# Issuing the scores of the next attention task before the PV of this one, and splitting each scan step into two group halves

## The chip, the cores and the metric

The kernel runs on the 8 cores of one Trainium2 chip. Each core computes 4 of the 32 sequences. The metric is device time in microseconds of the slowest core. PE is TensorE, PEld its weight loads, DVE VectorE, ACT ScalarE, POOL GpSimd and SP SyncE. A program on all cores also has a slower state, in which one die is granted a lower clock (in one run of e1 0.71 of full speed, against 0.77 on the other die); all comparisons here use fast runs only.

## The reference, cut to what matters

The model has four layers. Each runs a bidirectional complex-diagonal state-space scan beside a banded attention of window 128, and then a ConvFFN.

```python
# attention: 16 query blocks of 128, up to 3 key blocks each, 2 kv heads x 4 query heads
s = jnp.einsum('bnqkgd,bnskd->bnkgqs', q, kb) * (HEAD_DIM ** -0.5)
...
p = e / (jnp.sum(e, axis=-1, keepdims=True) + jnp.exp(sink_l - m))
o = jnp.einsum('bnkgqs,bnskd->bnqkgd', p, vb)
# scan, forward and reverse, 32 groups x 64 states
s_t = a * s_{t-1} + B u_t        # complex, real and imaginary parts kept apart
```

The kernel cuts the 2048 tokens into 64 chunks. Pass A (matrix multiplies) gives each chunk's contribution. The carry then runs through 64 dependent steps on DVE. Pass B adds the result back.

## The kernel before

Every instruction goes through a helper, which turns the buffers named as `reads` and `writes` into semaphore waits. A DVE operation that names a buffer which the previous DVE operation wrote waits for it, though both are on one engine. An attention "task" is one pair (query block `qb`, kv head `kv`).

```python
def att_block(qb):
    for kv in range(2):
        for kb in kbs:                       # 2 or 3 key blocks
            # S:   psum <- kT, qT                 PE   L822
            # exp: et   <- psum                   ACT  L825
            # pt   <- et * bias table             DVE  L827
        for c in range(4):                   # PV: 12 matmuls, PE L834
            ...
        # den <- psum + sink; den <- 1/den; oa <- psum*den     DVE L839, L841, L842
    # square of oa (ACT L845), 4 transposes (PE L849), copy to yaT (ACT L851)

def scan_step(c):      # L856 to L859; H is [128, 2 (re/im), 32 groups, 65 chunks]
    st1 = H[:, :, :, c] * aL[:, 0]           # every operation names the same buffer,
    H[:, :, :, c + 1] += st1                 # so each one waits for the one before it
    st1 = H[:, ::-1, :, c] * aL[:, 1]
    H[:, :, :, c + 1] += st1

for qb in range(8):                          # first half of the stage
    att_block(qb)
    passA_batch(4 * qb)      # 32 matmuls over 4 groups (L873); 2 mAb weight buffers from DRAM;
                             # two ACT copies put the result into H (L882, L883)
for qb in range(8, 16):                      # second half
    att_block(qb)
    for c in ...: scan_step(c)               # 8 steps a block
# then Ein <- H (DVE L896), pass B and the rest
```

The softmax here doesn't subtract the row's maximum and nothing guards it: scores larger than these inputs give would overflow.

## Time and profile before

| | |
|---|---|
| median before the change | 26421.76 us (6 runs) |
| the stage, first sequence: first H copy to Ein | 1143.22 to 1398.94 = 255.7 us, 16 times in the program |
| first half: pitch from block to block | 15.15 us on average |
| second half: pitch from block to block | 18.39 us is the usual value, 18.75 the longest |

Pitches are read from the timeline: in the first half the start of the first H copy of each block, in the second the start of every other reciprocal of den.

The overall view of the page, kernel before (the profiled run's span is 26406.8 us): busy us of each engine, share of the span, instructions.

```profile
PE 14588.9 (55%) x84876; PEld 8215.1 (31%) x84876; DVE 12674.6 (48%) x22475; ACT 8765.8 (33%) x14892; POOL 2825.2 (11%) x2532
```

No engine is near full, because the program is a row of stages with different limits. So the stage itself must be looked at. This is its window view, kernel before: the stretch and its length, then busy us of each engine with the instruction count, granted TensorE clock, DMA share and GB/s.

```profile
1143.22:1249.24 106.02, 58.48 (x463) 34.48 (x462) 28.54 (x84) 39.35 (x77) 0.00 (x0) 0.50 0.24 74
1249.24:1398.94 149.70, 47.36 (x262) 21.67 (x260) 98.04 (x351) 35.85 (x72) 0.00 (x0) 0.50 0.01 5
```

Nothing is full in the first half either: PE is busy 58 of 106 us. What bounds it is a chain through several engines. One stretch of the chain of waits, kernel before (start, length, what):

```profile
1207.89 0.55 PE psum L822
1208.64 0.61 ACT et_88 L825
1209.34 0.42 DVE pt_91 L827
...
1210.89 0.72 PE psum L834 x10
...
1212.93 1.09 PE psum L849 x4
...
1215.35 3.05 DMA mAb_84<-matsA
```

S, exp, multiply, PV and transposes follow each other, each begun when the one before has ended (the lines left out between PV and the transposes are den, its reciprocal and oa), and PE only works in between. The last line is a wait of PE for pass-A weights.

The second half is DVE's. Its timeline, kernel before, from the end of a scan into the attention work:

```profile
1325.06 0.27 DVE L858 TENSOR_TENSOR st_81<-H,aL 128x64 f32<-128x64 f32 x1
1325.43 0.28 DVE L859 TENSOR_TENSOR H<-H,st_81 128x64 f32<-128x64 f32 x1
1325.61 0.41 DVE L827 TENSOR_TENSOR pt_94<-et_88,eb 128x512 bf16<-128x512 bf16 x1
1325.94 0.42 DVE L827 TENSOR_TENSOR pt_95<-et_89,eb 128x512 bf16<-128x512 bf16 x1
...
1327.65 0.16 DVE L839 TENSOR_TENSOR den_98<-psum,esink 128x4 f32<-128x4 f32 x1 [0.96 <-PE psum L834]
...
1328.99 0.42 DVE L827 TENSOR_TENSOR pt_91<-et_88,eb 128x512 bf16<-128x512 bf16 x1 [0.36 <-ACT et_88 L825]
```

Two things are to be seen. The scan operations last 0.27 us but start every 0.37: each waits 0.10 for the one before. The multiplies after them last 0.42 but start every 0.33, because they do not depend on each other. And DVE stands idle (0.96 us for PV, 0.36 for exp, and 0.97 for the second PV, not shown).

### The profile page before, as it was taken

The numbers are of one execution on the slowest core, as the hardware profiler recorded it, in microseconds if no ns is written. First come the engines' busy times: TensorE is split into PE (matmuls) and PEld (weight loads), VectorE is DVE, ScalarE is ACT, GpSimd is POOL, SyncE is SP. The second block draws the span as 40 slices with busy tenths as digits, with TensorE's granted clock in tenths as the row PEclk, the third lists the DMA queues.
The fourth block names the chain that finished last, engine by engine and source line by source line (L and its number), as shares of the span: only waits on it lengthen the run. The fifth ranks groups of instructions, "written<-read, shape, count | busy, mean of one in ns | idle before, by whom it ended". The sixth has DMA issues, their size and how long they took to land.

```text
span 26406.8 us, 296755 instructions; the slowest of 8 cores (26307.9 to 26406.8 us)
## 1 busy us (share of the span) xinstructions
PE 14588.9 (55%) x84876; PEld 8215.1 (31%) x84876; DVE 12674.6 (48%) x22475; ACT 8765.8 (33%) x14892; POOL 2825.2 (11%) x2532
## 2 busy tenths in 40 slices
PE   1355437777235553777724555377772445537777
PEld 0222214444122221444412222244441222224444
DVE  7533435555653333555564333355557443335555
ACT  1333323444133332434413333244341333324443
POOL 1100001111210000111120000011112000001111
PEclk8666669999656666999965666699996566669999
DMA  0232231111022323111102222311110222231111
GB/s 28 71 90 86 85 115 42 36 38 40 33 66 90 90 87 119 34 37 40 34 33 71 85 90 90 117 37 39 35 38 33 81 76 84 90 117 40 40 37 35
DMA packets 664396, 1668.09 MB, mean 63 GB/s; under 512 B 115568, under 2 KB 248352, under 8 KB 654496
## 3 DMA queue, kind: packets, MB, share of 16 engines
q1 hardware_dynamic: 643808, 1558.92, 18.8%
q10 hardware_dynamic: 19008, 90.19, 1.1%
q8 instruction: 737, 12.08, 0.2%
q14 instruction: 843, 6.91, 0.1%
HBM read 1211.89 MB, written 436.99 MB: 62 GB/s over the span
## 4 chain that ended last, share of the span: by engine, by line
DVE 32%; PE 22%; DMA 19%; issue 13%; ACT 12%; DVEq 1%; ACTq 1%; SPq 0%; POOL 0%; POOLq 0%
PE psum L1084 10%; PE psum L1172 4%; DVE qT L942 2%; DMA z_scr<-hTlo 2%; PE psum L918 2%; DMA UY<-u_scr 2%; PE psum L834 1%; DVEq L97 1%; ACT fjunk L1120 1%; DVE H L857 1%; DVE H L859 1%; PE psum L822 1%; PE psum L873 1%; PE psum L745 1%; DMA xt_680<-out 1%
## 5 line engine op out<-in xcount | busy, mean ns | idle before, releaser
L1172 PE MATMUL psum<-h2T,wu 128*128 128x386 bf16 (+1 forms) x33792 | 5306.1, 311 | 1627.3 <-DVE cv_606 L1182 140.5
L1172 PEld LDWEIGHTS psum<-h2T,wu 128*128 128x128 bf16 x33792 | 3170.4, 98 | 3764.8 <-issue 2281.7
L1084 PE MATMUL psum<-wd,gbuf 128*128 128x512 bf16 x9216 | 2151.0, 389 | 26.7 <-POOL gbuf L1188 26.7
L1084 PEld LDWEIGHTS psum<-wd,gbuf 128*128 128x128 bf16 x9216 | 923.6, 100 | 1185.4 <-issue 152.4
L822 PE MATMUL psum<-qT,kT 64*128 64x512 bf16 x1472 | 708.9, 614 | 0.0
L979 PE MATMUL psum<-wo,hThi 128*128 128x512 bf16 x2048 | 507.8, 393 | 324.8 <-DVE mt_783 L984 13.6
L1092 DVE RECIPROCAL fstd<-fstd 128x1 f32<-128x1 f32 x256 | 41.9, 164 | 1297.8 <-ACT fstd L1090 1290.8
L1088 ACT ACTIVATE fjunk<-psum 128x1024 bf16<-128x1024 f32 x256 | 261.5, 1022 | 1197.0 <-PE psum L1084 1197.0
L769 PE MATMUL psum<-hTlo,wi 128*128 128x512 bf16 x2304 | 612.0, 389 | 44.6 <-DVE hTlo L748 16.5
L769 PE MATMUL psum<-hThi,wi 128*128 128x512 bf16 x2304 | 606.1, 386 | 0.0
L973 PE MATMUL psum<-wo,qT 128*128 128x512 bf16 x2048 | 519.1, 399 | 133.6 <-ACT mt_128 L982 5.1
L922 ACT ACTIVATE hTlo<-psum 128x512 bf16<-128x512 f32 x256 | 152.9, 597 | 1233.8 <-PE psum L918 1233.6
L778 DVE CAST qT<-psum 128x512 bf16<-128x512 f32 x256 | 177.0, 691 | 797.3 <-PE psum L769 797.3
L904 DVE MEMSET psum<- 128x512 f32 x256 | 124.2, 485 | 663.7 <-ACT hTlo L922 655.8
L979 PEld LDWEIGHTS psum<-wo,hThi 128*128 128x128 bf16 x2048 | 192.8, 100 | 629.5 <-issue 447.0
L1188 POOL TENSOR_TENSOR gpre_597<-gg_610,cv_604 128x384 bf16<-128x384 f32 (+1 forms) x24 | 21.8, 907 | 3332.9 <-ACT gg_610 L1185 3332.9
L1188 POOL TENSOR_TENSOR gpre_395<-gg_408,cv_402 128x384 bf16<-128x384 f32 (+1 forms) x24 | 21.8, 907 | 3329.7 <-ACT gg_408 L1185 3329.7
L1188 POOL TENSOR_TENSOR gpre_799<-gg_812,cv_806 128x384 bf16<-128x384 f32 (+1 forms) x24 | 21.8, 907 | 3326.2 <-ACT gg_812 L1185 3326.2
L1188 POOL TENSOR_TENSOR gpre_193<-gg_206,cv_200 128x384 bf16<-128x384 f32 (+1 forms) x24 | 21.8, 907 | 3319.9 <-ACT gg_206 L1185 3319.9
L769 PEld LDWEIGHTS psum<-hTlo,wi 128*128 128x128 bf16 x2304 | 224.7, 100 | 344.0 <-issue 98.9
L973 PEld LDWEIGHTS psum<-wo,qT 128*128 128x128 bf16 x2048 | 194.2, 101 | 438.3 <-issue 260.9
L1143 ACT CAST h2T<-psum 128x512 bf16<-128x512 f32 (+1 forms) x272 | 155.3, 571 | 523.9 <-DVE h2T L1141 523.9
(1963 smaller groups left out, 33605.7 us busy)
## 6 DMA issues: line engine op xcount, KB each, us to landing
UY<-u_scr SPq DMA_DIRECT2D x128, 256.0 KB
z_scr<-hTlo SPq DMA_DIRECT2D x128, 256.0 KB
xt_73<-x SPq DMA_DIRECT2D x56, 512.0 KB
xt_275<-out SPq DMA_DIRECT2D x56, 512.0 KB
xt_477<-out SPq DMA_DIRECT2D x56, 512.0 KB
xt_679<-out SPq DMA_DIRECT2D x56, 512.0 KB
fxt_196<-out SPq DMA_DIRECT2D x55, 512.0 KB
fxt_197<-out SPq DMA_DIRECT2D x55, 512.0 KB
```

The costliest lines, as they stand in the source:

```text
L97: E.eng.wait_ge(sem, val)
L745: K.op(pe, lambda: nc.tensor.transpose(psum[:, b + c // 4, (c % 4) * 128:(c % 4 + 1) * 128], hs[i][:, c * 128:(c + 1) * 128], ident[:]), r ...
L769: K.op(pe, lambda: nc.tensor.matmul(psum[:, b, :], wi[:, k, m * 128:(m + 1) * 128], hT[k // 4][:, k % 4, tg * 512:(tg + 1) * 512], start=( ...
L822: K.op(pe, lambda: nc.tensor.matmul(psum[:, b, :], kT[rows, kb * 128:(kb + 1) * 128], qT[rows, :, qb * 128:(qb + 1) * 128], start=True, st ...
L834: K.op(pe, lambda: nc.tensor.matmul(psum[:, b, c * 65:(c + 1) * 65], pt[ip][:, c * 128:(c + 1) * 128], vaug[:, kb, kv, 0:65], start=(n_ == ...
L857: K.op(dve, lambda: V.tensor_tensor(out=H[:, :, :, c + 1], in0=H[:, :, :, c + 1], in1=st1[:], op=ALU.add), reads=[H_b, aL_b, Hf_b], writes ...
L918: K.op(pe, lambda: nc.tensor.matmul(o_, l_, r_, start=False, stop=(n_ == len(mm) - 1), skip_group_check=True), reads=[mBb_b[im]] + rd_, wr ...
L942: K.op(dve, lambda: V.tensor_tensor(out=nat(ysT), in0=X1[:, m, tg * 512:(tg + 1) * 512].rearrange("p (s sub) -> p s sub", s=2), in1=gate[i ...
L973: K.op(pe, lambda: nc.tensor.matmul(psum[:, ba + hf, :], ysT[:, k, tt * 128:(tt + 1) * 128], wo[:, k, hf * 512:(hf + 1) * 512], start=(k = ...
L979: K.op(pe, lambda: nc.tensor.matmul(psum[:, bb_ + hf, :], yaT[:, k, tt * 128:(tt + 1) * 128], wo[:, 4 + k, hf * 512:(hf + 1) * 512], start ...
L1084: K.op(pe, lambda: nc.tensor.matmul(psum[:, b + hf, :], gt_[:, gi_, ti * 128:(ti + 1) * 128], wd[:, fb, hf * 512:(hf + 1) * 512], start=(f ...
L1172: K.op(pe, lambda: nc.tensor.matmul(psum[:, b, 0:nW], wu[:, k, rb * 128:(rb + 1) * 128], h2T[:, k, w0c:w1c], start=(k == 0), stop=(k == 7) ...
```

## The change

The intent is to give each in-order engine other work while a chain is in flight. Attention is cut into three parts: `att_S` (S, exp, multiply), `att_P` (PV, den, oa) and `att_F` (square, transposes, copy). The S part of the next task is issued before the PV part of this one, and the final part one task later. The scan step works on two halves of the groups in alternation.

```diff
-        for qb in range(NT // 2):
-            att_block(qb)
-            passA_batch(4 * qb)
+        tasks = [(qb, kv) for qb in range(NT) for kv in range(2)]
...
+        cur = att_S(*tasks[0])
+        fin = None
+        for ti, (qb, kv) in enumerate(tasks):
+            nxt = att_S(*tasks[ti + 1]) if ti + 1 < len(tasks) else None
+            att_P(qb, kv, cur)
+            cur = nxt
+            if fin is not None:
+                att_F(fin)
+                fin = None
+            if kv == 1:
+                fin = qb
+                if qb < NT // 2:
+                    passA_batch(4 * qb)
+                else:
+                    for c in ...: scan_step(c)
+        att_F(fin)
...
         def scan_step(c):
-            (four full-width operations, all on Hf_b)
+            hs_ = (slice(0, NG // 2), slice(NG // 2, NG))
+            hb_ = (Hf_b, Hb_b)
+            for (in_sw, ai) in ((False, 0), (True, 1)):
+                for h2 in range(2):      # st1[:, :, gs] = src * aL[:, ai, :, gs],      buffer hb_[h2]
+                    ...
+                for h2 in range(2):      # H[:, :, gs, c + 1] += st1[:, :, gs],          buffer hb_[h2]
+                    ...
```

More of the change, by code (lines that the diff above doesn't have):

```diff
@@ L811, in mixer_phase, with att_S @@
             print("mixer sbuf bytes remaining", nc.sbuf_bytes_remaining)
-        def att_block(qb):
+        def att_S(qb, kv):
             kbs = [kb for kb in (qb - 1, qb, qb + 1) if 0 <= kb < NT]
-            for kv in range(2):
-                rows = slice(kv * 64, (kv + 1) * 64)
-                pts = []
-                for kb in kbs:
-                    ie = K_rr(K, "et", 3)
-                    ip = K_rr(K, "pt", 6)
-                    b = next_ps()
-                    K.op(pe, lambda: nc.tensor.matmul(psum[:, b, :], kT[rows, kb * 128:(kb + 1) * 128],
-                                                      qT[rows, :, qb * 128:(qb + 1) * 128], start=True, stop=True),
-                         reads=[kT_b, qT_b], writes=[ps_b[b]])
-                    K.op(act, lambda: nc.scalar.activation(out=et[ie][:], in_=psum[:, b, :], func=AF.Exp, scale=0.125),
-                         reads=[ps_b[b]], writes=[et_b[ie]])
-                    K.op(dve, lambda: V.tensor_tensor(out=pt[ip][:], in0=et[ie][:],
-                                                      in1=eb[:, kb - qb + 1, kv].rearrange("p c q -> p (c q)"), op=ALU.mult),
-                         reads=[et_b[ie], ebB], writes=[pt_b[ip]])
-                    pts.append((ip, kb))
-                b = next_ps()
-                for c in range(4):
-                    for n_, (ip, kb) in enumerate(pts):
-                        K.op(pe, lambda: nc.tensor.matmul(psum[:, b, c * 65:(c + 1) * 65], pt[ip][:, c * 128:(c + 1) * 128],
-                                                          vaug[:, kb, kv, 0:65], start=(n_ == 0), stop=(n_ == len(pts) - 1)),
-                             reads=[pt_b[ip], va_b], writes=[ps_b[b]], inc=(c == 3 and n_ == len(pts) - 1))
-                io = qb % 2
-                ov = psum[:, b, 0:260].rearrange("p (c d) -> p c d", c=4)
-                K.op(dve, lambda: V.tensor_tensor(out=den[kv][:], in0=ov[:, :, 64], in1=esink[:, kv * 4:(kv + 1) * 4], op=ALU.add),
-                     reads=[ps_b[b], pb], writes=[den_b[kv]])
-                K.op(dve, lambda: V.reciprocal(out=den[kv][:], in_=den[kv][:]), reads=[den_b[kv]], writes=[den_b[kv]])
-                K.op(dve, lambda: V.tensor_tensor(out=oa[io][:, kv * 256:(kv + 1) * 256].rearrange("p (c d) -> p c d", c=4),
-                                                  in0=ov[:, :, 0:64], in1=den[kv][:].unsqueeze(2).to_broadcast([128, 4, 64]),
-                                                  op=ALU.mult), reads=[ps_b[b], den_b[kv]], writes=[oa_b[io]])
@@ new lines, in att_S @@
+            rows = slice(kv * 64, (kv + 1) * 64)
+            pts = []
+            for kb in kbs:
+                ie = K_rr(K, "et", 3)
+                ip = K_rr(K, "pt", 6)
+                b = next_ps()
+                K.op(pe, lambda: nc.tensor.matmul(psum[:, b, :], kT[rows, kb * 128:(kb + 1) * 128],
+                                                  qT[rows, :, qb * 128:(qb + 1) * 128], start=True, stop=True),
+                     reads=[kT_b, qT_b], writes=[ps_b[b]])
+                K.op(act, lambda: nc.scalar.activation(out=et[ie][:], in_=psum[:, b, :], func=AF.Exp, scale=0.125),
+                     reads=[ps_b[b]], writes=[et_b[ie]])
+                K.op(dve, lambda: V.tensor_tensor(out=pt[ip][:], in0=et[ie][:],
+                                                  in1=eb[:, kb - qb + 1, kv].rearrange("p c q -> p (c q)"), op=ALU.mult),
+                     reads=[et_b[ie], ebB], writes=[pt_b[ip]])
+                pts.append((ip, kb))
@@ new lines, in att_S, with att_P @@
+            return pts
+        def att_P(qb, kv, pts):
+            b = next_ps()
+            for c in range(4):
+                for n_, (ip, kb) in enumerate(pts):
+                    K.op(pe, lambda: nc.tensor.matmul(psum[:, b, c * 65:(c + 1) * 65], pt[ip][:, c * 128:(c + 1) * 128],
+                                                      vaug[:, kb, kv, 0:65], start=(n_ == 0), stop=(n_ == len(pts) - 1)),
+                         reads=[pt_b[ip], va_b], writes=[ps_b[b]], inc=(c == 3 and n_ == len(pts) - 1))
+            io = qb % 2
+            ov = psum[:, b, 0:260].rearrange("p (c d) -> p c d", c=4)
+            K.op(dve, lambda: V.tensor_tensor(out=den[kv][:], in0=ov[:, :, 64], in1=esink[:, kv * 4:(kv + 1) * 4], op=ALU.add),
+                 reads=[ps_b[b], pb], writes=[den_b[kv]])
+            K.op(dve, lambda: V.reciprocal(out=den[kv][:], in_=den[kv][:]), reads=[den_b[kv]], writes=[den_b[kv]])
+            K.op(dve, lambda: V.tensor_tensor(out=oa[io][:, kv * 256:(kv + 1) * 256].rearrange("p (c d) -> p c d", c=4),
+                                              in0=ov[:, :, 0:64], in1=den[kv][:].unsqueeze(2).to_broadcast([128, 4, 64]),
+                                              op=ALU.mult), reads=[ps_b[b], den_b[kv]], writes=[oa_b[io]])
@@ L845, in att_block, with att_F @@
+        def att_F(qb):
+            io = qb % 2
             K.op(act, lambda: nc.scalar.activation(out=junk[:, 0:512], in_=oa[io][:], func=AF.Square, accum_out=ssq[:, 2, qb:qb + 1]),
@@ L855, in scan_step @@
         def scan_step(c):
-            K.op(dve, lambda: V.tensor_tensor(out=st1[:], in0=H[:, :, :, c], in1=aL[:, 0], op=ALU.mult), reads=[H_b, aL_b, Hf_b], writes=[Hf_b])
-            K.op(dve, lambda: V.tensor_tensor(out=H[:, :, :, c + 1], in0=H[:, :, :, c + 1], in1=st1[:], op=ALU.add), reads=[H_b, aL_b, Hf_b], writes=[Hf_b])
-            K.op(dve, lambda: V.tensor_tensor(out=st1[:], in0=H[:, ::-1, :, c], in1=aL[:, 1], op=ALU.mult), reads=[H_b, aL_b, Hf_b], writes=[Hf_b])
-            K.op(dve, lambda: V.tensor_tensor(out=H[:, :, :, c + 1], in0=H[:, :, :, c + 1], in1=st1[:], op=ALU.add), reads=[H_b, aL_b, Hf_b], writes=[Hf_b])
+            hs_ = (slice(0, NG // 2), slice(NG // 2, NG))
+            hb_ = (Hf_b, Hb_b)
+            for (in_sw, ai) in ((False, 0), (True, 1)):
+                for h2 in range(2):
+                    gs = hs_[h2]
+                    src = H[:, ::-1, gs, c] if in_sw else H[:, :, gs, c]
+                    K.op(dve, lambda: V.tensor_tensor(out=st1[:, :, gs], in0=src, in1=aL[:, ai, :, gs], op=ALU.mult),
+                         reads=[H_b, aL_b, hb_[h2]], writes=[hb_[h2]])
+                for h2 in range(2):
+                    gs = hs_[h2]
+                    K.op(dve, lambda: V.tensor_tensor(out=H[:, :, gs, c + 1], in0=H[:, :, gs, c + 1], in1=st1[:, :, gs], op=ALU.add),
+                         reads=[H_b, aL_b, hb_[h2]], writes=[hb_[h2]])
         K.op(dve, lambda: V.memset(H[:, :, :, 0:1], 0.0), writes=[H_b, Hf_b, Hb_b])
@@ L887, in mixer_phase @@
         mA_load(1)
-        for qb in range(NT // 2):
-            att_block(qb)
-            passA_batch(4 * qb)
+        tasks = [(qb, kv) for qb in range(NT) for kv in range(2)]
         spq = NCH // (NT // 2)
-        for qb in range(NT // 2, NT):
-            att_block(qb)
-            for c in range((qb - NT // 2) * spq, (qb - NT // 2 + 1) * spq):
-                scan_step(c)
-        K.op(dve, lambda: V.tensor_copy(out=Ein[0:64], in_=H[0:64, :, :, 0:NCH]), reads=[H_b, Hf_b], writes=[Ein_b])
-        K.op(act, lambda: nc.scalar.copy(out=Ein[64:128], in_=H[64:128, :, :, 0:NCH][:, :, :, ::-1]), reads=[H_b, Hf_b], writes=[Ein_b])
+        cur = att_S(*tasks[0])
[12 more added lines that the diff above has]
+                else:
+                    for c in range((qb - NT // 2) * spq, (qb - NT // 2 + 1) * spq):
+                        scan_step(c)
+        att_F(fin)
+        K.op(dve, lambda: V.tensor_copy(out=Ein[0:64], in_=H[0:64, :, :, 0:NCH]), reads=[H_b, Hf_b, Hb_b], writes=[Ein_b])
+        K.op(act, lambda: nc.scalar.copy(out=Ein[64:128], in_=H[64:128, :, :, 0:NCH][:, :, :, ::-1]), reads=[H_b, Hf_b, Hb_b], writes=[Ein_b])
         def mB_load(g):
```

## The prediction

> **What bounds the kernel now.** The profile's overall view: span 26406.8 us, PE busy 55%, DVE 48%, ACT 33%; no engine bounds the whole, so only the stage touched counts: attention interleaved with the scan, once per sequence and layer (16 times). The timeline of the first sequence puts it at 1125.7 to 1398.9 us, 273 us, 16.5% of the span over 16. Window view there: PE clock 0.50, PE busy 61 of 111 us in the first half, DVE 96 of 144 in the second.
>
> First half (attention block plus pass-A batch; timeline, chain of waits): block 0 cannot start its batch before 1138.4 (UY and mAb transfers). Then 7 pitches of 15.1 us: two S, exp, multiply, PV passages of 4.3 and 3.7 us in which PE waits (S to first exp 0.8, exp pitch 0.49, multiply to PV), about 2 us for den, oa and transposes, and a batch of about 5.2, of which some 2.5 is one mAb transfer. That wait stays.
>
> Second half: pitch 18.39 us, all DVE: attention 6.64, scan 11.75 (32 operations of 0.27, pitch 0.37: each waits 0.10 for the one before).
>
> **What the change does.** No arithmetic is added in attention. S of the next task is issued ahead of PV of this one, the final transposes a task later.
> - First half: block becomes PE's own sum: S 2 x 1.3, PV 2 x 0.65, transposes 0.7, batch 5.2 = 9.8 us. Exp (behind the two H copies) still reaches PV in about 3.7 us after S, and PE has 3.9 us of other work. Saves 5.3 x 7 = 37 us per sequence; block 0 saves nothing (the transfer ends at the same time).
> - Second half, attention: the waits for PV and exp leave DVE; six multiplies at pitch 0.33 and two den chains of 0.9 give about 3.95 instead of 6.64. Saves 2.7 a block.
> - Scan: 64 half operations instead of 32. Trace: contiguous 128x32 f32 takes 0.193, and the strided 128x64 costs 0.04 over the (N+151)/0.96 form given for fp32 tensor_tensor in the Trainium skill, "VectorE: DVE Perf Modes", section on the TRN2 errata (which fits 3360 elements, 3657 ns, here). So a half takes about 0.213. With two chains the pair takes 0.213 + 0.10, so 0.157 each: 10.0 us instead of 11.75; I allow 10.3. The same page, section "The DRAIN you can't avoid", says to reduce op count and that the next op waits for the pipe; here independent multiplies of 0.42 start every 0.33, so overlap exists but is small. Scan gain: about 1.5 a block, the uncertain term.
>
> Second half saves (2.7 + 1.5) x 8 = 33 us. Other stages stay.
>
> **Sum.** 70 us x 16 = 1120 us: 26420 to about 25290 us, 4.3%. Range 24980 to 25620. Faster by over 2%: 0.94; within 2%: 0.05; slower: 0.01.
>
> **What would show it.** Timeline: first-half pitch 9.5 to 10.3; PE waits for PV nearly gone, the mAb wait left; scan half operations at pitch 0.15 to 0.17; second-half pitch near 14.3; stage near 203 us.
>
> **What would make it wrong.** If half operations cannot overlap (pitch 0.31), the scan takes 20 us a block and eats the gain; at 0.19 it is a small loss (total about 25550). If denser PE work lifts the clock above 0.5, the first half gains up to 1.4 us a block more (total near 25100). If exp comes later than PV, PE waits again.

## The result

The changed kernel takes 25298.45 us (median of 10 runs, 25291.89 to 25315.72). Before it was 26417.81 us (median of 20 runs). The ratio is 0.9577, with a 95% interval of 0.9569 to 0.9585. A ratio is the mean time of one kernel's fast runs over that of the other's of the same rounds, so it is not quite the ratio of these medians. Executions in which one die ran at a lower clock are left out of the means. The median stands 1119 us below before.

The overall view (span of the profiled run 25342.4 us) and the window view of the same stage, changed kernel:

```profile
PE 14426.2 (57%) x84876; PEld 8160.8 (32%) x84876; DVE 12808.3 (51%) x26571; ACT 8705.6 (34%) x14892; POOL 2823.7 (11%) x2532
```

```profile
1146.71:1216.54 69.83, 52.12 (x463) 31.52 (x462) 27.30 (x84) 37.06 (x78) 0.00 (x0) 0.50 0.37 114
1216.54:1331.60 115.06, 43.59 (x263) 21.16 (x261) 106.69 (x603) 34.56 (x72) 0.00 (x0) 0.50 0.02 6
```

The same work now takes 69.8 + 115.1 = 184.9 us instead of 106.0 + 149.7 = 255.7. That is 70.8 us a sequence and layer, and 16 x 70.8 = 1133 us. Summed over all 16 stages of the two traces, the stage went from 4094 to 2953 us, which is 1141 us less, against 1119 measured in the medians: the whole gain is in this stage. In the second half DVE is now busy 107 of 115 us. The clock stayed at 0.50, in this sequence and in the first halves of the other 15.

A whole block of the first half in the chain of waits, changed kernel:

```profile
1166.27 1.39 PE psum L821 x3
1167.66 0.77 PE psum L836 x12
1168.43 0.91 PE psum L854 x4
1169.34 1.39 PE psum L821 x3
1170.73 0.78 PE psum L836 x12
1171.50 0.47 PE psum L885 x8
...
1172.05 2.57 DMA mAb_83<-matsA
...
1176.08 1.39 PE psum L821 x3
```

ACT and DVE have left the chain. S (L821), PV (L836), the transposes of the block before (L854), S, PV and pass A (L885) follow each other on PE without a gap; one transfer is left. From S at 1166.27 to S at 1176.08 it is 9.81 us.

The timeline of DVE, changed kernel, for the same passage as before:

```profile
1247.25 0.40 DVE L866 TENSOR_TENSOR st_81<-H,aL 128x32 f32<-128x32 f32 x2
1247.57 0.41 DVE L870 TENSOR_TENSOR H<-H,st_81 128x32 f32<-128x32 f32 x2
1247.88 0.41 DVE L826 TENSOR_TENSOR pt_91<-et_88,eb 128x512 bf16<-128x512 bf16 x1
...
1248.89 0.15 DVE L841 TENSOR_TENSOR den_98<-psum,esink 128x4 f32<-128x4 f32 x1
...
1251.64 0.32 DVE L866 TENSOR_TENSOR st_81<-H,aL 128x32 f32<-128x32 f32 x2
```

The idle time before den is gone, as PV was done during the scan, and no line left out carries such a mark: attention takes 1247.88 to 1251.64 = 3.76 us. A pair of half operations ("x2") starts every 0.316 us, so one every 0.158. Eight of them make a step of 1.264 us instead of 4 x 0.3725 = 1.49.

### The profile page after: what moved, and what is told of

Read it like the earlier page. It is cut to its first block, busy times and chain, and to the rows that moved or that the text cites. A ratio compares the mean times of both kernels' runs of the same rounds, so it can differ in the third digit from the quotient of the medians.

```text
span 25342.4 us, 305891 instructions; the slowest of 8 cores (25110.5 to 25342.4 us)
## 1 busy us (share of the span) xinstructions
PE 14426.2 (57%) x84876; PEld 8160.8 (32%) x84876; DVE 12808.3 (51%) x26571; ACT 8705.6 (34%) x14892; POOL 2823.7 (11%) x2532
## 4 chain that ended last, share of the span: by engine, by line
DVE 31%; PE 22%; DMA 20%; issue 13%; ACT 12%; DVEq 1%; ACTq 1%; SPq 0%; POOL 0%; POOLq 0%
PE psum L1107 10%; PE psum L1195 4%; DVE qT L965 2%; PE psum L941 2%; DMA z_scr<-hTlo 2%; DMA UY<-u_scr 2%; DVE H L870 2%; PE psum L821 1%; ACT fjunk L1143 1%; DVEq L97 1%; PE psum L885 1%; DMA xt_477<-out 1%; PE psum L836 1%; PE psum L745 1%; DMA xt_275<-out 1%
## 5 line engine op out<-in xcount | busy, mean ns | idle before, releaser
L821 PE MATMUL psum<-qT,kT 64*128 64x512 bf16 x1472 | 688.1, 605 | 0.0
```

What stands on the lines that cost most here:

```text
L821: K.op(pe, lambda: nc.tensor.matmul(psum[:, b, :], kT[rows, kb * 128:(kb + 1) * 128], qT[rows, :, qb * 128:(qb + 1) * 128], start=True, st ...
```

## The experiments

The ten runs were made in three, each on one chip: e1 to e4, e5 to e8, then e9 and e10. These chips granted less clock (0.73 in the profiled run of e2, against 0.76 for before above), so medians are higher and the intervals of the ratios wider, about 0.003 to 0.007 to each side. Ratios to the kernel before of the same call are therefore compared, and the pitches of the traces, which hardly move with the clock where DVE is the limit. "H to Ein" is the length of the second half, from the last first-H-copy to Ein. "16 stages" is the time from the first H copy to Ein, summed over all 16 stages of the trace. Lines and buffers in their traces can have shifted numbers. All ten were correct.

| kernel | ratio to before | first-half pitch | second-half pitch | H to Ein | 16 stages |
|---|---|---|---|---|---|
| before | 1 | 15.15 | 18.39 | 149.7 | 4094 |
| the change | 0.9577 | 9.98 | 14.18 | 115.1 | 2953 |
| e10, the change again | 0.9586 | 10.05 | 14.19 | 115.2 | 2957 |
| e1 | 0.9663 | 10.11 | 15.5 | 126.9 | 3146 |
| e2 | 0.9958 | 15.36 | 17.05 | 138.1 | 3906 |
| e3 | 0.9884 | 10.09 | 20.9 | 169.7 | 3836 |
| e4 | 0.9700 | 12.43 | 14.18 | 114.5 | 3211 |
| e5 | 0.9408 | 6.50 | 14.18 | 115.1 | 2595 |
| e6 | 0.9562 | 10.15 | 14.0 | 114.3 | 2944 |
| e7 | 0.9458 | 9.88 | 11.84 | 97.6 | 2680 |
| e8 | 0.9302 | 6.49 | 11.83 | 97.5 | 2330 |
| e9 | 0.9505 | 10.40 | 12.6 | 103.0 | 2771 |

(First-half pitch is the mean of 7, the second-half pitch the usual value of one sequence, both of the first sequence like H to Ein; all in us.)

The theory: the gain is two separate sums. In the first half the chain S, exp, multiply, PV is replaced by PE's own work plus one transfer. In the second half the waits leave DVE, and the alternation of halves hides each operation's wait for the one before. The rivals: the scan split is the main gain; shorter operations gain by themselves; the order of the final part does not matter.

### e1: attention pipelining alone

```diff
-  scan_step of the changed kernel (half operations)
+  scan_step of the kernel before (four full-width operations)
```

> Only the attention pipelining, with the old scan step (four full-width operations in one chain). Theory A (two additive parts): first half as in the changed kernel (pitch 9.8 us), second-half pitch 3.8 + 11.75 = 15.5 us instead of 14.2, so 1.33 us x 8 blocks x 16 = 170 us slower than the changed kernel: about 25470 us, ratio to before 0.964. Rival B (the scan split is what gains, the pipelining mostly moves waits): above 26000 us.

Measured: ratio 0.9663 (0.9633 to 0.9693). First half as in the change. Second-half pitch 15.5 to 15.6 us as forecast. The second half is 126.9 - 115.1 = 11.8 us longer than in the change, 189 us in 16 sequences. Against e10 the ratio is 0.0077 higher, 203 us on 26418. So most of the gain is the pipelining. Rival B falls.

### e2: scan split alone

```diff
-  scan_step of the kernel before (four full-width operations)
+  scan_step of the changed kernel (half operations); attention order as before
```

> Only the scan split, with the old attention order. Theory A: scan of a block 10.4 instead of 11.75 us, nothing else moves, so 170 us faster than before: about 26250 us, ratio 0.9935, second-half pitch 17.0 us. Rival B: far more than that, below 25900 us. Rival C (the gain of the split exists only with the pipelining): 26420 us.

Measured: ratio 0.9958 (0.9932 to 0.9985), 111 us; the forecast 0.9935 is just inside the interval. The second half is 149.7 - 138.1 = 11.6 us shorter, 186 us in 16, and its pitch is 17.05. The first half is unchanged within its scatter. This is the same gain as e1 lacks (11.8), so the two parts add. Over all 16 stages e1 saves 948 us and e2 188, together 1136, and the change 1141. The ratios alone are too wide to show it: 3.4% and 0.4% against 4.2%.

### e3: the same half operations, not in alternation

```diff
-            for (in_sw, ai) in ...:
-                for h2 in range(2):  multiply of half h2
-                for h2 in range(2):  add of half h2
+            for h2 in range(2):
+                for (in_sw, ai) in ...:
+                    multiply of half h2
+                    add of half h2
```

> The changed kernel, same 64 half operations a block, but each half runs its four operations one after the other instead of alternating with the other half. Theory A (the pitch is set by the wait of an operation for the one before it, and alternation hides it): pitch 0.31 instead of 0.158 us, scan of a block about 20 us, total about 25300 + 64 x 8 x 0.155 x 16 = 26570 us, slower than before. Rival B (shorter operations gain by themselves, or the pitch of 0.158 is an issue limit): 25300 us.

Measured: ratio 0.9884 (0.9851 to 0.9917), so about 790 us above the change (0.9884 - 0.9586 on 26418), not the 1270 forecast. The direction is theory A's and the size is a miss. The timeline of DVE in e3 shows why:

```profile
1244.26 0.22 DVE L868 TENSOR_TENSOR H<-H,st 128x32 f32<-128x32 f32 x1
1244.39 0.20 DVE L866 TENSOR_TENSOR st<-H,aL 128x32 f32<-128x32 f32 x1
1244.69 0.22 DVE L868 TENSOR_TENSOR H<-H,st 128x32 f32<-128x32 f32 x1
```

Where the next operation depends on the last, it starts 0.30 to 0.32 us after it. Where the other half begins, it starts after 0.13. I had forgotten that two of the eight starts of a step change to the other half. A step is 6 x 0.312 + 2 x 0.125 = 2.12 us, and 64 x (2.12 - 1.264) x 16 = 877 us. Rival B falls: the same operations in this order are slower than the undivided ones of e1 (pitch 20.9 against 15.5). The alternation is what gains. And 0.158 is no issue limit, since 0.125 is seen here.

### e4: the final part of a block not delayed

```diff
             att_P(qb, kv, cur)
             cur = nxt
-            if fin is not None:
-                att_F(fin)
-                fin = None
             if kv == 1:
-                fin = qb
+                att_F(qb)
```

> The changed kernel with the final square and transposes of a block issued right after its last PV, ahead of the pass-A batch, instead of one task later. Theory A: PE waits some 1.4 us for den and oa in each of 7 first-half blocks, and nothing is lost in the second half where DVE is the chain: 1.4 x 7 x 16 = 160 us slower than the changed kernel, about 25460 us, ratio to before 0.9635. Rival B (the delay is irrelevant, the mAb transfer absorbs it): 25300 us.

Measured: ratio 0.9700 (0.9669 to 0.9731). First-half pitch 12.43 instead of 9.98: 2.45 x 7 x 16 = 274 us (258 over all 16 stages); the second half does not change. The delay matters more than forecast. The transposes of a final part in the timeline of e4:

```profile
1180.63 1.09 PE L854 MATMUL psum<-ident,oa 128*128 128x128 f32 x4 [2.16 <-DVE oa L844]
```

PE waits 2.16 us for oa, not 1.4. I took 1.4 from the kernel before, where den follows PV at once. In the new order DVE first has the three multiplies of the next task in its queue, and den stands behind them. So issuing S ahead alone already gains (12.43 against 15.15), but its full worth needs the delay of the final part: the two belong together.

### e5: four pass-A weight buffers

```diff
-        mAb = [... for i in range(2)]     # index g % 2, load of g + 2
+        mAb = [... for i in range(4)]     # index g % 4, load of g + 4; the unused st2 is dropped for room
```

> The changed kernel with four mAb buffers instead of two (the unused st2 tile is dropped for room). Theory A (the first half is PE's own sum plus one transfer of 2.6 us a block that PE waits for in the open): pitch 9.8 to 7.2 us, 2.6 x 7 x 16 = 290 us faster than the changed kernel, about 25010 us, ratio to before 0.947; a little less again if the granted clock rises above 0.5. Rival B (the transfers are limited by bandwidth, or ACT and DVE are next behind PE): pitch above 8.5 us, above 25150 us.

Measured: ratio 0.9408 (0.9366 to 0.9449). The first stage to Ein takes 160.64 us instead of 184.89. It is one of the shortest, so it must not be multiplied by 16: over all 16 the saving is 2953 - 2595 = 358 us (the table's sums), more than the 290 forecast. Pitches of 7.13 and of 6.0 us occur. The windows of e5 tell them apart (same columns as above):

```profile
1159.00:1184.00 25.00, 22.02 (x276) 15.13 (x273) 15.40 (x48) 21.43 (x45) 0.00 (x0) 0.98 0.56 171
1184.00:1199.00 15.00, 15.00 (x135) 9.09 (x133) 8.37 (x26) 11.24 (x24) 0.00 (x0) 0.50 0.69 211
```

At clock 0.50 PE is busy all of 15.00 us, and the pitch is 7.13, where 7.2 was forecast. At clock 0.98 the pitch is 6.0, and ACT (21.43 of 25.00) is almost as busy as PE (22.02). The transfers reach 211 GB/s, so bandwidth was not the limit. Theory A holds. In the one stage whose first half stayed at 0.50 throughout, that half took 49.9 us, against 69.7 on average in the change; 16 such stages would save 316 us. So some 40 of the 358 us go with the higher clock, which the forecast named as a possibility but did not size.

### e6: full-width scan step with two temporaries

```diff
-  half operations in alternation
+  st1 = H[:, :, :, c] * aL[:, 0]         # reads Hf_b, writes st_b[0]
+  st2 = H[:, ::-1, :, c] * aL[:, 1]      # reads Hf_b, writes st_b[1]
+  H[:, :, :, c + 1] += st1               # reads st_b[0], writes Hf_b
+  H[:, :, :, c + 1] += st2               # reads st_b[1], writes Hf_b
```

> The changed kernel with a full-width scan step again, but with two temporaries, so that the two multiplies of a step do not wait for each other. Theory A (only waits for the operation just before cost time): a step is 3 waited pitches of 0.37 = 1.11 us instead of 1.264, 64 x 0.155 x 16 = 160 us faster than the changed kernel, about 25140 us, ratio to before 0.9515. Rival B (splitting by halves is needed): a step stays at 1.49 us as in before, about 25530 us.

Measured: ratio 0.9562 (0.9525 to 0.9600), second-half pitch 14.0: the same as the change, neither theory's number. The timeline of DVE in e6:

```profile
1243.24 0.27 DVE L860 TENSOR_TENSOR st<-H,aL 128x64 f32<-128x64 f32 x1
1243.42 0.26 DVE L861 TENSOR_TENSOR st<-H,aL 128x64 f32<-128x64 f32 x1
1243.79 0.27 DVE L862 TENSOR_TENSOR H<-H,st 128x64 f32<-128x64 f32 x1
...
1244.54 0.27 DVE L860 TENSOR_TENSOR st<-H,aL 128x64 f32<-128x64 f32 x1
```

The second multiply does start 0.18 us after the first. But the first add starts 0.37 after the second multiply. It needs only the first. The helper makes it wait because the second multiply reads the buffer `Hf_b` that the add writes, though they touch different columns. A step is 1.30 us.

### e9: the same, with the dependency tracked by column parity

```diff
+  src_b, dst_b = (Hf_b, Hb_b)[c % 2], (Hf_b, Hb_b)[(c + 1) % 2]
   # both multiplies read src_b, both adds write dst_b
```

> As e6 (full-width step, two temporaries), but the dependency of H is tracked by column parity, so that the first add no longer waits for the second multiply, which only reads the old column. In e6's trace the first add started 0.36 us after the second multiply, not 0.37 after the first. Theory A (e6 missed its forecast through that needless wait alone): the second multiply hides inside the wait of the first, a step is 3 x 0.373 = 1.12 us against 1.30 in e6 and 1.264 in the changed kernel; second-half pitch 13.0 us; 147 us faster than e10, ratio to e10 about 0.994. Rival (a full-width add waits for whatever was issued last, needed or not): a step 1.30, pitch 14.0 as in e6.

Measured: ratio to before 0.9505 (0.9438 to 0.9572), to e10 0.9505 / 0.9586 = 0.9916. The timeline of DVE in e9:

```profile
1245.87 0.27 DVE L862 TENSOR_TENSOR st<-H,aL 128x64 f32<-128x64 f32 x1
1246.06 0.25 DVE L863 TENSOR_TENSOR st<-H,aL 128x64 f32<-128x64 f32 x1
1246.24 0.27 DVE L864 TENSOR_TENSOR H<-H,st 128x64 f32<-128x64 f32 x1
...
1247.00 0.27 DVE L862 TENSOR_TENSOR st<-H,aL 128x64 f32<-128x64 f32 x1
```

The first add now starts 0.18 after the second multiply. A step is 1.13 us, and the second half is 115.2 - 103.0 = 12.2 us shorter than in e10 (194 us in 16; 147 were forecast). So the needless wait explains e6. The pitch fell to 12.6 where the forecast said 13.0: a part of this surplus may lie in the stall described under "Why the prediction was right", which this kernel with its fewer instructions meets less often; no run tests it. With four operations a step, this form beats the change's eight, and halving is one way to hide the wait, not the only one. The ratios of e9 and e10 overlap in their intervals; the verdict rests on the traces.

### e7: one multiply for both products

```diff
-  two multiplies a half: H * aL[:, 0] and H[:, ::-1] * aL[:, 1]
+  one multiply a half: st4[:, s, r] = H[:, s] (broadcast over r) * aX[:, s, r]
+  aX[:, s, r] = aL[:, (s + r) % 2, r], made once a sequence; then two adds a half, in alternation
```

> The changed kernel with both multiplies of a half made one operation (H broadcast against a rearranged coefficient tile), so 6 instead of 8 half operations a step, in alternation as before. Theory A: a step is (0.26 + 0.10) + 2 x 0.316 = 0.99 us instead of 1.264, 64 x 0.27 x 16 = 280 us faster than the changed kernel, about 25020 us, ratio to before 0.947. Rival B (the multiply of 64 elements costs twice that of 32): a step 1.26 us, 25300 us.

Measured: ratio 0.9458 (0.9418 to 0.9499), second-half pitch 11.84. The first stage to Ein is 184.89 - 166.70 = 18.19 us shorter than in the change, and all 16 together 273 us; 280 were forecast. A step in its timeline of DVE:

```profile
1252.04 0.44 DVE L870 TENSOR_TENSOR st<-H,aX 128x64 f32<-128x64 f32 x2
1252.41 0.72 DVE L875 TENSOR_TENSOR H<-H,st 128x32 f32<-128x32 f32 x4
1253.05 0.45 DVE L870 TENSOR_TENSOR st<-H,aX 128x64 f32<-128x64 f32 x2
```

A step is 1253.05 - 1252.04 = 1.01 us, with the pair of multiplies at 0.37 and two pairs of adds at 0.32 each. Rival B falls.

### e8: e5 and e7 together

```diff
+  four mAb buffers (e5) and one multiply a half (e7); st4 and aX are views of the idle tile xt[2], for room
```

> Four mAb buffers and the one multiply together (temporaries in an idle xt tile for room). Theory A: the two gains lie in different halves of the stage and add: 25300 - 290 - 280 = 24730 us, ratio to before 0.936. Rival B (transfers or the clock take part of it back): 24850 us or more.

Measured: ratio 0.9302 (0.9266 to 0.9338). The first stage to Ein is 184.89 - 142.94 = 41.95 us shorter than in the change, and all 16 together 623 us; the parts alone gave 358 + 273 = 631. They add, as they lie in different halves. This version beats both kernels.

### e10: the change again

> The changed kernel unaltered, on the same chip and in the same call as e9, because the chips of the first two calls granted a lower clock than the one on which the result was taken. Theory: the ratio to before is 0.9577 again, within its interval of some 0.003 on such a chip, though both medians are higher; first-half pitch 9.8 to 10, second-half 14.2 us.

Measured: ratio 0.9586 (0.9548 to 0.9623), second-half pitch 14.19. The result holds on a chip with a lower clock.

## Why the prediction was right

The predicted 25290 us and the measured 25298 us agree better than any single term does. The terms, per sequence or block:

| term | predicted | measured |
|---|---|---|
| first block: nothing saved (from the u_scr transfer to the first H copy) | 0 | 47.3 to 46.5 us |
| first-half pitch | 9.8 | 9.77 to 9.85 for five of seven, mean 9.98 |
| first half, 7 pitches | saves 37 | 36.2 (106.0 - 69.8) |
| attention on DVE, second half | 6.64 to 3.95 | 3.76 |
| half operation, alone and as pitch | 0.213, 0.157 | 0.208 to 0.215, 0.158 |
| scan of a block | 11.75 to 10.3 | 10.42 (14.18 - 3.76) |
| second half | saves 33 | 34.6 (149.7 - 115.1) |
| sum x 16 | 1120 | 1133 from the first stage, 1141 over all 16, 1119 in the medians |

- **The bound was read from the right place.** The shares of busy time (55% and 48%) said nothing. The chain of waits in the first half and the DVE timeline in the second did. That the first half would become PE's own sum is shown by the chain of the changed kernel, and by e5, where taking out the one remaining wait leaves PE busy 15.00 of 15.00 us.
- **The mAb wait stays, block 0 saves nothing.** Both came true (block 0 saved 0.8 us). In the two long pitches of the first half (10.25 and 10.53 us) the transfer took longer.
- **The scan term was the uncertain one.** The prediction reasoned that with two chains a pair costs one operation plus its wait. e3 shows the alternation to be the cause, and e6, e9 and e7 show that the same arithmetic of waits forecasts other step forms, once every wait is counted, the helper's needless one too.
- **The trace was rightly put above the page on the pipe drain.** The Trainium skill, "VectorE: DVE Perf Modes", section "The DRAIN you can't avoid", says that the next operation does not start until the pipe is empty. It adds that one which is not held starts earlier, which the prediction does not mention. By the first sentence alone, twice the operations would have been a loss. The overlap seen in this trace (0.42 us operations starting every 0.33) said otherwise. The same page, section "Rules for kernel authors", advises fewer operations. That is not refuted here: once the waits were hidden, e9 with four operations a step and e7 with six beat the change with eight.
- **The clock did not rise.** It was named as a risk; it stayed 0.50 in the changed kernel and rose only in e5 and e8, where the transfer wait of PE was gone.

Small errors partly cancelled: attention came 0.19 us a block better, the scan 0.12 and the mean first-half pitch 0.18 worse. Inside the first-half pitch there was luck as well. By the chain above, S took 2.78 us a block (2.6 predicted), PV 1.55 (1.3), the transposes 0.91 (0.7) and the batch with its transfer 4.58 (5.2): the four errors sum to 0.02 us. The mechanism was right, the sizes of its terms were not.

The scan's remainder is known in place but not in cause. 64 x 0.158 = 10.1 us, and about once a block DVE stands idle for 0.25 to 0.35 us where the usual wait is 0.10 or less. Such a place in the timeline of DVE, changed kernel:

```profile
1230.86 0.33 DVE L866 TENSOR_TENSOR st_81<-H,aL 128x32 f32<-128x32 f32 x2
1231.55 0.33 DVE L870 TENSOR_TENSOR H<-H,st_81 128x32 f32<-128x32 f32 x2 [0.35 <-DVE st_81 L866]
```

Numbering DVE's instructions in the trace from its start, waits included, shows where it happens. Between two scan operations of this trace there are 125 stalls of over 0.17 us, and each comes at an instruction whose number, divided by 128, leaves 59 or 60. In the other eleven traces it is 59, 60 or 61. So the stall goes with the number of instructions. What stops DVE there is not shown. The change raised DVE's instructions from 52120 to 60216, waits included; e9 has 52136, and 54 such stalls.

## What to carry to other kernels

In a stage where no engine is full, write down the chain of one iteration and the sum of each engine alone; the gap is what software pipelining can give, and the largest single sum plus the waits that remain is the new pitch. For a recurrence of small operations on one engine, count waited starts, not operations: interleave a second independent chain, or give independent operations of a step their own temporaries, and check that the dependency helper does not add waits for parts that do not overlap. When work is issued ahead on one engine, everything behind it in the other queues comes later, so the consumers there must be moved back too.

## What the Trainium skill lacked or had wrong

- "VectorE: DVE Perf Modes", section "The DRAIN you can't avoid", reports of eight tensor_copy in a row that leaving out the semaphores between them gains nothing. Here a waited start costs: 128x64 f32 operations start every 0.37 us when each waits for the one before, and 0.18 us after one that they need not wait for (e9). With the same four operations a step went from 1.49 to 1.13 us.
- No page has measured start-to-start times, without a wait, of Vector operations as short as these. The runs show 0.125 us for 128x32 f32 (e3) and 0.18 for 128x64 f32 (e9).
- The form (N+151)/0.96 that "VectorE: DVE Perf Modes", section on the TRN2 errata, gives for fp32 tensor_tensor is called exact at 512 and 2048 elements. The trace of the kernel before extends this to contiguous tiles of 3360 elements (3657 ns) and, within 3 ns, of 32 (193 ns against 191).
- "TensorE: Matmul & The Clock Gate", Part 1, says that some 3.4 us of sustained activity release the throttle. In e5 PE was busy 15.00 of 15.00 us (as the profile models it) with a granted clock of 0.50, just after 25 us at 0.98. No run here tells what set it back.
